# Moving the second MLP's tokens from byte 448 to byte 256 of each chunk of the activations

## The chip, the cores and the metric

The kernel runs on one core of a Trainium2 chip. The metric is the time of one execution on the device, in microseconds; the runs before the change are given as the median of three.

The engines are named as the profile names them: PE is TensorE's matmuls, PEld its weight loads, DVE is VectorE, ACT is ScalarE, POOL is GpSimd, SP is the queue that issues most transfers.

## The reference

Two transformer layers over 256 latent tokens and 256 context tokens of width 1024, batch 1. Layer 0 mixes with a retention scan, layer 1 with neighbourhood attention; both are followed by an MLP with 4096 hidden columns. The result is the latent tokens after layer 1.

```python
def sq_relu_mlp(h, w1, w2):
    return jnp.square(jax.nn.relu(h @ w1)) @ w2

# in each layer i, behind its mixer's output y:
x = layer_norm(DN_ALPHA * x + g1 * y, ln_g[i, 0], ln_b[i, 0])
h = x * (1.0 + sc2) + sh2
x = layer_norm(DN_ALPHA * x + g2 * sq_relu_mlp(h, mlp_w1[i], mlp_w2[i]), ln_g[i, 1], ln_b[i, 1])
```

In layer 0 the context tokens go through the MLP as well; in layer 1 only the 256 latent tokens do. The change concerns `h` of layer 1's MLP, "the second MLP".

## The kernel before

**Numbers in two parts.** Every matrix product is made of three matmuls on operands split into a high part (rounded to the chip's `float32r`) and a low part (the rest): high x high, high x low and low x high (`mm3`). Weights arrive by transfers of 512 KB (`fetch`, on the SP queue) into tiles `raw`; ScalarE casts them to `hi`, VectorE subtracts to get `lo` (`lows`). They are consumed in a fixed order (`take`).

**The activations.** The modulated tokens that a layer's products read stand transposed in two tiles, `hTh` (high) and `hTl` (low), of shape 128 partitions x 8 chunks x 512 columns. A chunk holds 128 of the 1024 features, one per partition, and its 512 columns are tokens: 2048 bytes in each partition. `hs(k, a, b)` gives columns a to b of chunk k of both. In the first MLP and in layer 1's mixer columns 0 to 255 are latent tokens and 256 to 511 context tokens.

**The second MLP's tokens.** They are only 256, so half of each chunk stays unused. `AT` (line 1928) is the column of the first of them, and `toks(t)` the columns of token tile t (128 tokens). `LINE` is 16 columns, 64 bytes. The columns are written by `affine_half` for token tile 0 (a ScalarE cast into `hTh`, a VectorE subtraction into `hTl`) and by `direct` for token tile 1.

**How they are read.** The first product of the second MLP has two forms:

- Hidden columns 0 to 511 (block 0) are made with the tokens as stationary operand, loaded as weights of 128 columns, and the MLP's weights as moving operand of 256 columns (`tok_part`, tiles `p1t`): 96 matmuls, interleaved by hand with the layer norm of the second token tile. Their results are transposed by `turn_block` (tiles `pt`).
- Hidden columns 512 to 4095 (blocks 1 to 7, the loop over `f4`) are made by `mm1`, with a 128 x 128 block of the MLP's weights as stationary operand and all 256 tokens as moving operand. Per block there are two halves `f2`, per half two groups of 128 hidden columns, 8 chunks and three matmuls: 7 x 2 x 2 x 8 x 3 = 672 matmuls into PSUM tiles that the profile calls `p`.

The first MLP calls the same `mm1` with `at=0`: for its first two blocks with the 256 latent tokens alone, then with all 512.

```python
def hs(k, a, b):
    return hTh[:, k, a:b], hTl[:, k, a:b]

def mm1(us, sl, pb, ks=range(KC), at=0):
    for i in range(2):
        for k in ks:
            wh, wl = us[k // 4]
            mm3(
                pb[i][:, sl], (wh[:, k % 4, tsl(i)], wl[:, k % 4, tsl(i)]),
                hs(k, at + sl.start, at + sl.stop), k == 0, k == KC - 1,
            )
```

A weight tile here is 128 partitions x 4 x 256 columns of 4 bytes, so the slice `wh[:, k % 4, tsl(i)]` starts 1024 (k % 4) + 512 i bytes into the tile. In the program's address map `hTh` starts at byte 40608 of each partition, `hTl` at 56992, and the five `hi` tiles at 97952 and steps of 4096 from there: all of them 160 bytes past a multiple of 512, as are the `lo` tiles.

**Order.** From the end of the mixer to the opening of the second MLP's loop the order of the instructions on PE, ACT, DVE and POOL is the written one; inside the loop the scheduler of the language orders what is ready. Behind the first product the second one (`mm2b`) reads the hidden values, not `hTh` or `hTl`, and the last layer norm and the output's transfers end the kernel.

Of the kernel before, what the change touches and what calls it, by code (L numbers as in the profile page):

```python
# [36 lines left out]
LINE = 16  # L37
# [67 lines left out]
def kernel(  # L105
# [50 lines left out]
    def bank(s="ps"):  # L156
        return psp.tile([P, 512], F32, tag="ps", name=nm(s))

    def slot(i, shape, dt, s):

        return arena.tile(shape, dt, tag=f"s{i}", name=nm(s))
# [1087 lines left out]
# [8 lines that stand above are left out]
# [668 lines left out]

    AT = 7 * LINE
    ht = slot(N_Q, [P, 4, 2, NLAT], F32R, "hid1")
    us4 = take(2, 0, 1)  # L1930

    def toks(t):
        return slice(AT + t * P, AT + (t + 1) * P)

# [126 lines left out]
    for f4 in range(1, 8):  # L2061
        ht = slot(HS1[f4], [P, 4, 2, NLAT], F32R, "hid1")
        for f2 in range(2):
            opening = f4 == 1 and f2 == 0
            us = take(2, 0, 2) if opening else take(2)
            pb = [bank("p1") for _ in range(2)]
            mm1(us, LAT, pb, at=AT)
            dve.on = f4 < 3
# [144 lines left out]
```

## Time and profile before

| | |
|---|---|
| median of three runs | 1175.99 us |
| lowest, highest | 1175.35, 1176.32 us |
| the profiled execution | 1176.32 us |
| its span, first to last instruction | 1174.4 us |
| granted TensorE clock, mean | 0.998 |

How the rows of the profile are read. In a group of instructions "x224: 276/276/369" is the count and the minimum, median and maximum duration in ns, followed by the first and last start in us and the shapes. Rows of the timeline give start and duration in us. Matmuls are pipelined, so their durations overlap; the distance between two starts is the time that a matmul costs. Rows of a window give, for each engine, busy us and in brackets the number of instructions, then the granted clock, the busy share of the DMA engines and GB/s. Rows of the chain give start, length, and what the chain ran through. All rows carry line 84 (L84), the helper that records every operation, so tiles tell them apart.

### The profile page before, as it was taken

To read this page: it belongs to the slowest core of one execution; us is meant where nothing else is said; L and a number is where in the kernel's file an instruction comes from. 1 tells how busy PE (TensorE), PEld (TensorE's weight loads), DVE (VectorE), ACT (ScalarE), POOL (GpSimd) and SP (SyncE) were. 2 spreads that over 40 slices of the span, in tenths; PEclk is the share of its full clock that TensorE was granted. 3 is DMA by queue.
4 is the path that set the end of the run, shared out by engine and by line. 5 is a ranking of instruction groups with operands and counts; after the bars stand their busy time and mean duration, and the time that the engine had idled before them with its cause. 6 is when DMAs were issued, how large, how long until landed. Compare 5 with 4: busy or idle time off the path is not lost.

```text
span 1174.4 us, 17544 instructions
## 1 busy us (share of the span) xinstructions
PE 1161.8 (99%) x6687; PEld 980.7 (84%) x6687; DVE 848.4 (72%) x1361; ACT 481.1 (41%) x819; POOL 235.1 (20%) x418
## 2 busy tenths in 40 slices
PE   9999999999999999999999999999999999999997
PEld 6788888888888889888888888879778878999886
DVE  3786687777898787757777675578577589877456
ACT  3643332222323246441212333137466666756341
POOL 0102001010220241770312001223443430000001
PEclk9999999999999999999999999999999999999999
DMA  9943552544355426756556665646344335766760
GB/s 275 277 130 105 162 187 96 156 153 144 112 178 177 140 65 220 181 113 215 177 184 198 211 200 179 197 157 202 81 136 144 107 113 160 214 206 205 237 215 36
DMA packets 140115, 195.10 MB, mean 166 GB/s; under 512 B 9936, under 2 KB 81136, under 8 KB 140032
## 3 DMA queue, kind: packets, MB, share of 16 engines
q1 hardware_dynamic: 131904, 182.03, 49.8%
q0 software_dynamic: 6976, 9.39, 3.8%
q10 hardware_dynamic: 1152, 2.56, 0.7%
q8 instruction: 52, 0.85, 0.3%
q14 instruction: 31, 0.25, 0.1%
HBM read 189.12 MB, written 5.75 MB: 166 GB/s over the span
## 4 chain that ended last, share of the span: by engine, by line
PE 74%; DMA 12%; DVE 8%; issue 3%; ACT 2%; POOL 0%; DVEq 0%; ACTq 0%
PE p L84 23%; DMA rawa<-in_ada_w_dram 11%; PE pq L84 8%; PE pv L84 8%; PE pw L84 7%; PE pg L84 7%; PE pn L84 4%; DVE acc L84 4%; PE pnv L84 4%; PE po L84 3%; DVE lo L84 3%; PE pnw L84 1%; PE ppt L84 1%; PE pS L84 1%; PE pav L84 1%
## 5 line engine op out<-in xcount | busy, mean ns | idle before, releaser
L84 ACT CAST hi<-raw 128x1024 fp32r<-128x1024 f32 (+2 forms) x228 | 231.9, 1032 | 306.7 <-PE p L84 114.2
L84 DVE TENSOR_TENSOR lo<-raw,hi 128x1024 fp32r<-128x1024 f32 (+2 forms) x228 | 272.6, 1210 | 101.3 <-ACT hi L84 101.1
L84 PE MATMUL p<-hi,hid 128*128 128x512 f32 (+1 forms) x780 | 238.2, 386 | 0.0
L84 PEld LDWEIGHTS p<-hi,hid 128*128 128x128 f32 x780 | 145.7, 188 | 29.3
L84 PE MATMUL p<-hTl,hi 128*128 128x256 f32 (+1 forms) x512 | 165.9, 326 | 0.0
L84 PE MATMUL p<-hTh,lo 128*128 128x256 f32 (+1 forms) x512 | 165.9, 326 | 0.0
L84 PE MATMUL p<-hTh,hi 128*128 128x256 f32 (+1 forms) x512 | 162.6, 327 | 0.0
L84 PE MATMUL p<-lo,hid 128*128 128x512 f32 (+1 forms) x390 | 150.8, 387 | 2.1 <-DVE lo L84 2.1
L84 DVE SCALAR_TENSOR_TENSOR acc<-rawa,scol,acc 128x1024 f32<-128x1024 f32 x56 | 74.4, 1341 | 65.1 <-DMA rawa<-in_ada_w_dram 65.1
L84 PEld LDWEIGHTS p<-hTh,lo 128*128 128x128 f32 x512 | 96.3, 188 | 8.8
L84 PEld LDWEIGHTS p<-hTl,hi 128*128 128x128 f32 x512 | 96.4, 188 | 8.7
L84 PEld LDWEIGHTS p<-hTh,hi 128*128 128x128 f32 x512 | 94.3, 188 | 8.7
L84 PEld LDWEIGHTS p<-lo,hid 128*128 128x128 f32 x390 | 73.3, 188 | 17.9 <-DVE lo L84 3.2
L84 DVE SCALAR_TENSOR_TENSOR strips<-rawa,scol,strips 128x512 f32<-128x512 f32 x112 | 78.6, 764 | 0.0
L84 ACT CAST hid<-r 128x256 fp32r<-128x256 f32 (+1 forms) x64 | 31.9, 500 | 112.4 <-DVE r L84 112.3
L84 POOL TENSOR_TENSOR rstd<-rstd,misc 128x1 f32<-128x1 f32 x28 | 19.1, 684 | 216.5 <-DVE rstd L84 215.5
L84 ACT ACTIVATE s<-s,mn 128x512 f32<-128x512 f32 x64 | 45.5, 713 | 21.6 <-DVE mn L84 21.6
L84 PE MATMUL pw<-hi,oh 128*128 128x512 f32 x128 | 50.8, 397 | 0.0
L84 PE MATMUL pg<-hi,hTh 128*128 128x512 f32 x128 | 50.6, 395 | 0.0
L84 PE MATMUL pw<-hi,ol 128*128 128x512 f32 x128 | 50.0, 390 | 0.0
L84 PE MATMUL pg<-hi,hTl 128*128 128x512 f32 x128 | 49.9, 390 | 0.0
L84 PE MATMUL pw<-lo,oh 128*128 128x512 f32 x128 | 49.8, 389 | 0.0
(241 smaller groups left out, 2275.2 us busy)
## 6 DMA issues: line engine op xcount, KB each, us to landing
raw<-in_mlp_w_dram SPq DMA_DIRECT2D x128, 512.0 KB, 4.5
rawa<-in_ada_w_dram SPq DMA_DIRECT2D x80, 512.0 KB, 3.9
raw<-in_ret_w_in_dram SPq DMA_DIRECT2D x42, 512.0 KB, 4.0
raw<-in_nat_w_in_dram SPq DMA_DIRECT2D x24, 512.0 KB, 4.1
rawq<-in_ada_w_dram SPq DMA_DIRECT2D x16, 512.0 KB, 6.0
raw<-in_ret_w_o_dram SPq DMA_DIRECT2D x16, 512.0 KB, 3.5
bias<-rpb_rows POOLq DMA_DIRECT2D x32, 128.0 KB, 2.9
raw<-in_nat_w_o_dram SPq DMA_DIRECT2D x8, 512.0 KB, 3.7
```

Of the source, the lines that this page charges most:

```text
L84: r = f(*args, **kwargs)
```

## The change

`AT` goes from 7 lines to 4: the tokens start 256 bytes into each chunk in place of 448, as columns 64 to 319 in place of 112 to 367. Both tiles, all eight chunks, every write and every read of them go along. Nothing else differs.

```diff
-    AT = 7 * LINE
+    AT = 4 * LINE
     ht = slot(N_Q, [P, 4, 2, NLAT], F32R, "hid1")
     us4 = take(2, 0, 1)
```

## The prediction

> **What bounds the kernel now.** I read the page first (busy shares, granted clock), then the chain of waits over the last 174 us, because the changed offset is first used at about 988 us, then the two stages that read the moved tokens, tile by tile and in order of time.
>
> ```profile
> span 1174.4 us, 17544 instructions
> PE 1161.8 (99%) x6687; PEld 980.7 (84%) x6687; DVE 848.4 (72%) x1361; ACT 481.1 (41%) x819; POOL 235.1 (20%) x418
> ...
> 1002.74 5.66 PE p L84 x48
> 1008.40 0.44 PE pt L84 x4
> 1008.83 158.03 PE p L84 x1026
> 1166.87 0.02 issue
> ```
>
> TensorE is busy 99% of the span. The other rows are the chain in order of time: from 1002.74 to 1166.87 us it is TensorE alone (matmuls into `p`, once broken by four transposes), and behind that only a short settling of the last outputs. So a matmul that issues later in this stretch ends the kernel later, one for one.
>
> ```profile
> core 0: us, PE busy (x) PEld busy (x) DVE busy (x) ACT busy (x) POOL busy (x), PEclk, DMA share, GB/s
> 1010.00:1079.00 69.00, 69.00 (x611) 69.00 (x611) 54.64 (x84) 42.25 (x76) 0.00 (x0) 1.00 0.65 204
> ...
> L84 PE MATMUL p<-hTh,hi x224: 276/276/369, 1002.5 to 1079.1; 128*128 128x256 f32 x112
> ```
>
> This is the first product of the second MLP (blocks 1 to 7 of its hidden columns): 224 matmuls for each of the three pairs of high and low parts, of which the row shows one, 672 in all, of 256 tokens each, from 1002.5 us until the second product takes over at 1079.4. In the window TensorE never idles at a granted clock of 1.00, while VectorE is busy 54.64 of 69 us, ScalarE 42.25 and the DMA engines 0.65. The median duration is 276 ns, but matmuls overlap; what counts is the distance from start to start.
>
> **The change part by part.** The change alters one constant, so no instruction, DMA, queue entry or wait is added or removed. Every pair of accesses that overlapped before overlaps still (the earlier readers of these two tiles read all 512 token columns of a chunk), so the waits are the same. What moves is an address: columns 112 to 367 of each chunk become columns 64 to 319, 192 bytes lower. Four groups touch them.
>
> *1. The 672 matmuls, which stream these tokens as moving operand.* Each runs with a weight load of 128 columns beside it, out of a tile whose slices start at multiples of 512 bytes; in the program's address map the token tiles and all weight tiles of this product start 160 bytes past a multiple of 512. So the starts of the two streams differ by 448 modulo 512 now, and by 256 after. The first MLP runs the same form of matmul with the tokens at offset 0, which gives a pair of rows to compare: first the old stage at offset 0, then this one.
>
> ```profile
> 450.43 0.28 PE L84 MATMUL p<-hTh,lo 128*128 128x256 f32 x1
> ...
> 450.91 0.28 PE L84 MATMUL p<-hTh,lo 128*128 128x256 f32 x1
> ...
> L84 PE MATMUL p<-hTh,hi x27: 283/283/283, 447.1 to 455.0; 128*128 128x256 f32 x27
> L84 PEld LDWEIGHTS p<-hTl,hi x20: 192/192/192, 447.1 to 454.0; 128*128 128x128 f32 x20
> ```
>
> ```profile
> 1040.19 0.28 PE L84 MATMUL p<-hTh,lo 128*128 128x256 f32 x1
> ...
> 1041.89 0.28 PE L84 MATMUL p<-hTh,lo 128*128 128x256 f32 x1
> ...
> L84 PE MATMUL p<-hTh,hi x178: 276/276/276, 1011.7 to 1071.9; 128*128 128x256 f32 x178
> L84 PEld LDWEIGHTS p<-hTl,hi x177: 187/188/188, 1012.1 to 1071.9; 128*128 128x128 f32 x177
> ```
>
> At offset 0 four steps (450.43 to 450.91, three rows left out) take 0.48 us: 120 ns each, every matmul lasts 283 ns and every weight load 192. At offset 448 fifteen steps (1040.19 to 1041.89) take 1.70 us: 113.3 ns each, the matmul 276, the load 187 to 188. Same shape, same clock, no idle time in either: only the offset differs, and it is worth 6.7 ns per matmul. The rows at offset 0 also bound the pattern: that stage uses weight slices 0, 512, 1024 ... bytes into a tile, and minimum, median and maximum are all 283. So a shift of 512 bytes changes nothing, and only the offset modulo 512 can matter. One more row belongs here, from the start of the same stage, still at offset 448:
>
> ```profile
> 1005.05 0.28 PE L84 MATMUL p<-hTh,hi 128*128 128x256 f32 x1
> ...
> 1006.23 0.28 PE L84 MATMUL p<-hTl,hi 128*128 128x256 f32 x1
> ...
> L84 PE MATMUL p<-hTh,hi x13: 281/281/281, 1002.9 to 1007.2; 128*128 128x256 f32 x13
> ```
>
> Ten steps in 1.18 us are 118 ns (the chain's first piece, 48 matmuls in 5.66 us, says the same: 117.9), at 281 ns a matmul. So 448 itself has two rhythms: the first 48 matmuls run in the slow one, and behind the four transposes at 1008.4 us the other 624 run in the fast one. Which one is taken seems to hang on how the two streams stand to one another when TensorE starts afresh.
>
> What 256 does, no row shows; I bound it. From below: transposes of 128 columns load the same number of weight columns, and their rhythm is the least one that any full-width load shows.
>
> ```profile
> 1002.14 0.60 PE L84 MATMUL pt<-cst,r 128*128 128x128 f32 x4
> ...
> L84 PE MATMUL pt<-cst,r x8: 270/272/273, 1002.1 to 1008.6; 128*128 128x128 f32 x8
> ```
>
> Four of them span 0.60 us, the last of which lasts 0.272, so three steps take 0.33 us: 109 ns. From above: 120 ns, the slowest steady rhythm that a matmul of 256 tokens has anywhere in the trace. Between 109 and 120 I take 120. The fewest assumptions that give 448 a gain over 0 are that the two streams disturb each other by place, in a pattern that repeats after some number of bytes. It repeats at 512. If it also repeats at 256 or 128, then 256 is the same as 0, while 448, which is a multiple of 64 alone, remains different. Only if it repeats at 512 and nowhere below is 256 a new case. The row that 256 is nearest to is the one at offset 0.
>
> The cost: 624 x 6.7 ns = 4.2 us, and 48 x (120 - 117.9) = 0.1 us. All of it is on the chain.
>
> [...]
>
> *2. The 96 matmuls of block 0, which load these tokens as weights* (moving the weights of the model instead, 989 to 1002 us).
>
> ```profile
> 989.38 0.62 PE L84 MATMUL p1t<-hi,hTh 128*128 128x256 f32 x4
> 989.84 0.62 PE L84 MATMUL p1t<-lo,hTh 128*128 128x256 f32 x4
> 990.29 0.96 PE L84 MATMUL p1t<-hi,hTh 128*128 128x256 f32 x7
> ...
> L84 PE MATMUL p1t<-hi,hTh x32: 276/279/392, 989.4 to 998.7; 128*128 128x256 f32 x32
> ```
>
> Eight steps from 989.38 to 990.29 take 0.91 us, again 113 to 114 ns; the median over all is 279 ns, so most run near the 281 of the slow rhythm. At 120 ns some 16 matmuls lose 6.7 ns and 80 lose about 2.1: 0.3 us. At the floor of 109 they would gain 16 x 4.3 + 80 x 8.9 = 0.8 us.
>
> *3. The writes into the moved columns.*
>
> ```profile
> L84 ACT CAST hTh<-aff x2: 621/622/622, 987.8 to 989.9; 128x512 fp32r<-128x512 f32 x2
> ...
> L84 ACT CAST hTh<-aff x8: 601/618/641, 783.3 to 807.6; 128x512 fp32r<-128x512 f32 x8
> ```
>
> At 448 the cast takes 621 ns; the same form in the second layer's mixer, at other columns, takes 618. Medians 3 ns apart: I cost these two at nothing, and with them the four subtractions and the eight small affine writes of the second token tile; at 3 ns each all 14 are under 0.05 us either way.
>
> *4. What runs beside it.* A slower TensorE gives the weight transfers, casts and subtractions more room, so no wait arises. A faster one would ask 4% more of engines that are busy at most 79% in that window; nothing new is late there. The second product that follows, up to 1166.9 us, does not read these tiles and moves as a block.
>
> The sum is 4.2 + 0.1 + 0.3 = 4.6 us. The profiled execution took 1176.32 us (1.9 us around its span of 1174.4), which gives 1180.9; it is the highest of the three runs, 0.33 above their median of 1175.99, so I predict 1180.6 us, 0.4% slower. The three runs lie within 0.08%; I count 0.2% (2.35 us) as what can be told from no change.
>
> **The rivals.**
> *Offset 256 behaves as 448 does.* Any offset that is no multiple of 512 may part the two streams as well. For it: 448 helps in two roles, as moving operand (1040 us) and as weights (989 us), where the shift has the opposite sign, so the gain does not hang on one direction. Against it: two rhythms at one and the same offset show that details matter. Time: 1176.0; if all 672 take the fast rhythm, 48 x 4.6 ns = 0.2 less. [...]
> *Offset 256 keeps the streams apart for good.* In one step of 120 ns 256 columns are streamed and 128 loaded, so the moving stream reads at twice the pace of the weight stream: from equal starts it is a whole 512-byte turn ahead just as both end, and meets the other stream at each boundary. Started half a turn apart they would meet only in mid-stream. The point that decides is whether such a meeting costs under 4 ns. Price: 624 x 4.3 + 48 x 8.9 = 3.1 us, with part 2's 0.8 in all 3.9 us: 1172.1, down to which the other engines in the window keep up. [...]
> *Offset 256 locks into the slow rhythm throughout*: 624 x 4.6 = 2.9 us, 1178.9.
> *The mid-stream meeting is expensive*, the moving stream being held behind the slower one: beyond 120 ns, which no row of the trace shows; each 10 ns would be 6.7 us.
>
> **How the numbers follow.** As offset 0 (1180.6): 0.46. As 448 (1176.0): 0.25. Floor or near it (1172.1 to 1173.6): 0.18. Slow rhythm throughout (1178.9): 0.07. Beyond 120 ns: 0.04. The likeliest case alone lies within 1179.9 to 1181.3 (the three runs' spread to both sides). The cases have both signs, so the range goes from the floor case to that upper end, 1172.0 to 1181.3, and leaves out only the last. Slower by over 0.2%: 0.46 + 0.07 + 0.04 = 0.57; within 0.2%: 0.25 and a little of the floor case that stops short, 0.27; faster: 0.16.
>
> **What would show it.** In the stage after 1002 us, start to start of 120 ns, matmuls of 283 ns and loads of 192 show the first step right; 276 and 113.3 show the first rival, 272 to 273 and 109 the second, 281 the third. The stage of 672 should last 81 us in place of 76.9, and everything before 988 us and each step behind the stage should keep its length. The prediction is wrong if the pattern of the two streams has no period below 512 bytes.

## The result and the profile after

| | before | after |
|---|---|---|
| median of seven runs | 1175.64 us | 1180.94 us |
| lowest, highest | 1172.57, 1177.92 us | 1177.42, 1182.74 us |
| the profiled execution, its span | 1176.32, 1174.4 us | 1182.74, 1180.8 us |

The ratio is 1.0040 with a 95% interval of 1.0026 to 1.0054: 3.1 to 6.3 us slower. On every engine the instructions are the same, in number and in order.

The page of the changed kernel opens with its span and the busy shares:

```profile
span 1180.8 us, 17544 instructions
PE 1168.2 (99%) x6687; PEld 986.2 (84%) x6687; DVE 849.5 (72%) x1361; ACT 482.9 (41%) x819; POOL 234.9 (20%) x418
```

TensorE's matmuls are busy for 6.4 us more, as much as the span grew; VectorE and ScalarE gained 1.1 and 1.8 us. Where the 6.4 us lie is read from the chain of waits, in order of time (start, length, what), first of the kernel after, then the rows of the kernel before that the prediction did not show:

```profile
988.75 2.87 PE pnw L84 x24
991.62 1.92 PE p1t L84 x16
...
993.57 1.79 PE p1t L84 x12
...
996.35 8.16 PE p1t L84 x68
1004.51 0.44 PE pt L84 x4
1004.94 5.76 PE p L84 x48
1010.70 0.44 PE pt L84 x4
1011.14 162.18 PE p L84 x1026
```

```profile
986.67 2.89 PE pnw L84 x24
...
990.39 1.06 ACT hi L84
...
991.49 1.78 PE p1t L84 x12
...
994.28 8.03 PE p1t L84 x68
```

The last piece grew from 158.03 to 162.18 us. It holds 624 matmuls of the moved tokens and 402 of the second product, so that is 4.15 / 624 = 6.65 ns for each of the 624. The first 48 grew from 5.66 to 5.76 us, block 0's 68 from 8.03 to 8.16. The transposes between them kept their 0.44. That makes 4.4 us. Block 0's first 28 matmuls add almost nothing: from the end of `pnw` to the piece of 68 it is 4.72 us before and 4.73 after. In the kernel before TensorE waited behind the first 16 of them for a cast on ScalarE (`ACT hi`); after, the 16 run longer and the wait is gone. The remaining 2 us are there before the changed offset is used: this execution enters the chain at 988.75 in place of 986.67. They are taken up below.

The stage itself, by a window, by tile, and in order of time, as the prediction read it of the kernel before:

```profile
1012.00:1085.00 73.00, 73.00 (x610) 73.00 (x609) 56.00 (x85) 44.83 (x78) 0.00 (x0) 1.00 0.64 196
```

```profile
L84 PE MATMUL p<-hTh,hi x181: 283/283/283, 1014.9 to 1079.7; 128*128 128x256 f32 x181
L84 PEld LDWEIGHTS p<-hTl,hi x181: 192/192/192, 1014.9 to 1079.7; 128*128 128x128 f32 x181
```

```profile
1040.00 0.28 PE L84 MATMUL p<-hTh,lo 128*128 128x256 f32 x1
...
1041.80 0.28 PE L84 MATMUL p<-hTh,lo 128*128 128x256 f32 x1
```

Still no idle time at a granted clock of 1.00, and VectorE, ScalarE and the transfers are about as busy as before (77, 61 and 64% against 79, 61 and 65%). Fifteen steps take 1.80 us in place of 1.70: 120.0 ns each, every matmul 283 ns, every load 192. These are the numbers of the first MLP at offset 0, to the nanosecond.

**The 2 us that are not the change's.** Both executions wait near 768 us for the low part of a weight tile, behind late transfers of weights: the cast on ScalarE that comes ahead of it waited 4.97 us for its transfer before and 5.43 us after. The chain just behind the waits, before and then after:

```profile
770.33 9.62 PE p L84 x41
```

```profile
769.44 12.55 PE p L84 x47
```

The two pieces do not begin at the same matmul, since the kernel before waits a second time, shortly. The matmul that starts at 768.23 us before starts at 769.44 after, 1.2 us later; 0.56 us of that is the longer idle stretch ahead of it, the rest was there before. At the transposes at the end of these pieces, 779.94 and 781.98 us, the kernel after is 2.04 us late. The windows show where the other 0.8 us come from (the seventh figure behind the stretch, ahead of the DMA share, is the granted clock), before and then after; below them are the rows of the two waits:

```profile
768.20:770.30 2.10, 1.66 (x6) 1.05 (x6) 1.96 (x7) 1.05 (x1) 0.51 (x1) 1.00 1.02 289
```

```profile
766.00:769.40 3.40, 1.17 (x6) 0.63 (x4) 3.34 (x6) 1.04 (x1) 0.00 (x0) 1.00 0.70 197
769.40:772.80 3.40, 3.36 (x8) 2.69 (x9) 3.26 (x8) 1.04 (x1) 0.51 (x1) 0.51 0.91 289
```

```profile
768.23 0.50 PE L84 MATMUL p<-lo,hid 128*128 128x512 f32 x1 [1.70 <-DVE lo L84]
```

```profile
769.44 0.79 PE L84 MATMUL p<-lo,hid 128*128 128x512 f32 x1 [2.26 <-DVE lo L84]
```

Behind an idle stretch of 2.26 us the granted clock was 0.51 for 3.4 us, eight matmuls long; behind one of 1.70 us it stayed at 1.00. The wait lies in the first layer's MLP, which no moved column touches, and it is not in every run: in the profiled run of the experiment with a later break (below) one piece of the chain passes over the place, 161 matmuls in 36.50 us, the 226.7 ns of an unbroken stream.

The 2.26 us stand in a stretch of 3.40 us, 766.00 to 769.40, of which TensorE was busy for 1.17. In the profiled run of the experiment at 480 bytes (below) two waits in the same place, 1.9 us together and the longer one 1.4, left the clock at 1.00 in the windows from 764 to 776 us.

### The profile page after: what moved, and what is told of

It is laid out like the page before. It is cut to its first block, busy times and chain, and to the rows that moved or that the text cites. A ratio compares the mean times of both kernels' runs of the same rounds, so it can differ in the third digit from the quotient of the medians.

```text
span 1180.8 us, 17544 instructions
## 1 busy us (share of the span) xinstructions
PE 1168.2 (99%) x6687; PEld 986.2 (84%) x6687; DVE 849.5 (72%) x1361; ACT 482.9 (41%) x819; POOL 234.9 (20%) x418
## 4 chain that ended last, share of the span: by engine, by line
PE 74%; DMA 13%; DVE 8%; issue 2%; ACT 1%; SPq 1%; POOL 0%; DVEq 0%; ACTq 0%
PE p L84 24%; DMA rawa<-in_ada_w_dram 11%; PE pg L84 7%; PE pw L84 7%; PE pq L84 7%; PE pv L84 6%; PE pn L84 5%; PE pnv L84 4%; DVE acc L84 4%; PE po L84 3%; DVE lo L84 3%; PE ppt L84 2%; PE pnw L84 1%; PE pS L84 1%; PE pav L84 1%
## 5 line engine op out<-in xcount | busy, mean ns | idle before, releaser
L84 PE MATMUL pq<-hTh,hi 128*128 128x512 f32 x128 | 49.3, 395 | 0.8 <-ACT hTh L84 0.4
```

The lines of the kernel that those rows point to most:

```text
L84: r = f(*args, **kwargs)
```

## The experiments

The theory: what counts is the difference between the start of the moving operand and the start of the weights, in a pattern that repeats every 256 bytes. Its rivals: a pattern that repeats every 128 bytes; the place of the tokens alone, whatever the weights' place; and, for the two rhythms seen at 448, that the order of the work decides more than the bytes. No kernel here leaves out any computation. All edits are to the changed kernel, and each group was timed beside the kernel before on its chip (medians 1175.14, 1175.14 and 1175.47 us). "The stage" is the 672 matmuls; the chain's two pieces `p x48` and `p x1026` measure it, and per matmul the last 624 take 113.3 ns plus what the second piece has over 158.03 us, divided by 624.

**Offset 0: is 256 the same as 0?**

```diff
-    AT = 4 * LINE
+    AT = 0
```

> The changed kernel with the tokens at the start of each chunk. Theories A, A' and B: the same as 256, 120 ns in the stage of 672 and in block 0, matmuls of 283 ns, 1180.6 us, ratio to the kernel before about 1.004. If 256 and 0 differ by more than 0.1% or by more than 1 ns a matmul, the reading that 256 repeats 0 falls.

Measured: 1179.89 us, ratio 1.0044 (1.0025 to 1.0064). The chain, and the tile in the stage:

```profile
1005.81 5.76 PE p L84 x48
...
1012.01 162.18 PE p L84 x1026
```

```profile
L84 PE MATMUL p<-hTh,hi x154: 283/283/283, 1019.8 to 1074.8; 128*128 128x256 f32 x154
```

5.76 and 162.18 us, 283 ns: the same three numbers as at 256. A shift by 256 bytes changes none of them here.

**Offset 128: does the pattern repeat at 128?**

```diff
-    AT = 4 * LINE
+    AT = 2 * LINE
```

> The changed kernel with the tokens 128 bytes into each chunk in place of 256. Theory A (the moving stream and the weight load disturb each other by the difference of their starts, in a pattern that repeats every 128 bytes): as 256, 120 ns from start to start and matmuls of 283 ns in the stage of 672, time as the changed kernel, about 1180.6 us. Theory A' (the pattern repeats every 256 bytes, not every 128): 128 is a case of its own, at or below 118 ns, matmuls of 281 ns or less, 1176 to 1179 us. Theory B (where the tokens lie, not how they stand to the weights, sets it) leaves both open. Theory C (the state in which TensorE starts the stage picks the rhythm, the offset only tips it): a mix of 113, 118 and 120 ns within the stage.

Measured: 1180.27 us, ratio 1.0056 (1.0036 to 1.0075); the chain's second piece is 162.22 us, a mean of 120.0 ns. By the mean alone 128 would pass for 0. The tile, form by form, says otherwise:

```profile
L84 PE MATMUL p<-hTh,lo x84: 284/284/285, 1044.8 to 1074.6; 128*128 128x256 f32 x84
L84 PE MATMUL p<-hTh,hi x84: 285/285/285, 1044.9 to 1074.8; 128*128 128x256 f32 x84
L84 PE MATMUL p<-hTl,hi x84: 281/281/282, 1045.0 to 1074.9; 128*128 128x256 f32 x84
```

284, 285 and 281 ns in turn, where offset 0 has 283 for each; start to start the three steps take 118 to 122 ns. So the pattern does not repeat at 128, though the time is the same. Neither expectation came out whole: a pattern of 128 was to give 283 ns throughout, one of 256 at most 118 ns.

**Offset 64.**

```diff
-    AT = 4 * LINE
+    AT = 1 * LINE
```

> The changed kernel with the tokens 64 bytes into each chunk. Theories A and A': an odd multiple of 64 bytes, so 113.3 or 117.9 ns as at 448, and about 1176 us (1176 to 1179 if it stays in the 117.9 ns rhythm); if 448 was good because it is just below 512 and not because it is an odd multiple, 120 ns and 1180.6 us. Theory C: rhythm as in the changed kernel where the start of the stage is the same, 120 ns.

Measured: 1177.85 us, ratio 1.0025 (1.0011 to 1.0038).

```profile
993.39 7.87 PE p1t L84 x68
...
1001.70 5.66 PE p L84 x48
...
1007.79 160.81 PE p L84 x1026
```

```profile
L84 PE MATMUL p<-hTl,hi x157: 279/279/279, 1019.8 to 1074.9; 128*128 128x256 f32 x157
```

The second piece has 2.78 us more than at 448, 4.5 ns per matmul: all 672 run at 117.8 ns, the mean of the slow rhythm that 448 shows in its first 48 alone (though a matmul lasts 279 ns here and 281 there), and the transposes do not end it. Block 0, where the tokens are the weights, gains instead: 7.87 us for 68 matmuls, against 8.03 at 448 and 8.16 at 256. There the difference of the two streams has the opposite sign, so 64 stands in block 0 as 192 does in the stage, and 448 (192 modulo 256) as 64. For these 68 matmuls the order of the times is swapped with the roles: 115.7 ns on the mean at 64, 118.1 at 448. For block 0's first 16 it is not, here at 64:

```profile
988.50 0.63 PE L84 MATMUL p1t<-hi,hTh 128*128 128x256 f32 x4
...
989.44 1.90 PE L84 MATMUL p1t<-hi,hTh 128*128 128x256 f32 x12
```

Eight steps take 0.94 us, about 117.5 ns, where the prediction's rows of block 0 at 448 have 113 to 114. So the fast rhythm occurs at a difference of 64 too, and the difference alone does not say which of the two rhythms is taken.

**The weight tiles moved, the tokens left at 256.** A tile of 64 bytes ahead of the weight tiles shifts them, and what lies behind them, up by 64. The difference becomes 192 modulo 256, as it is at 448, while the tokens stay in their columns.

```diff
+    padp = ec(tc.tile_pool(name="padp", bufs=1))
     hip = ec(tc.tile_pool(name="hip", bufs=WB))
...
+    padp.tile([P, 16], F32, tag="pad", name="pad")
```

> The changed kernel, tokens still at 256, with 64 unused bytes ahead of the weight tiles, so that all weight tiles (and the tiles placed behind them) lie 64 bytes higher and the token tiles stay. Theory A and A' (the difference of the two starts counts): the stage of 672 goes back to 113.3 or 117.9 ns although the tokens lie where the changed kernel has them, and so does every other stage of 256 token columns against weights (120 ns before): minus 4 to 5 us there, and for the 512-column matmuls of the token tiles either nothing (226.7 ns) or up to 6.7 ns each (220 ns). Theory B (the tokens' own place counts): the stage of 672 stays at 120 ns and the time at 1180.6 us. Theory C: no rhythm changes but by chance.

Measured: 1184.3 us, ratio 1.0086 (1.0068 to 1.0103): slower than everything so far. The chain and the tile in the stage:

```profile
1012.75 5.66 PE p L84 x48
...
1018.84 158.04 PE p L84 x1026
```

```profile
L84 PE MATMUL p<-hTl,hi x163: 276/276/276, 1019.8 to 1074.9; 128*128 128x256 f32 x163
```

In the stage the kernel before is back: 5.66, then 158.04 us, 276 ns. The tokens' own place alone is not what counts. The loss lies elsewhere: the matmuls of 512 columns, in the first layer, now meet weights 64 bytes further on. In order of time, in the first MLP, before and then here:

```profile
469.80 0.39 PE L84 MATMUL p<-hTl,hi 128*128 128x512 f32 x1
...
473.88 0.39 PE L84 MATMUL p<-hTl,hi 128*128 128x512 f32 x1
```

```profile
469.81 0.39 PE L84 MATMUL p<-hTl,hi 128*128 128x512 f32 x1
...
474.01 0.39 PE L84 MATMUL p<-hTl,hi 128*128 128x512 f32 x1
```

Eighteen steps take 4.08 us before, 226.7 ns each, and 4.20 us here, 233.3. The same move that is worth 6.7 ns to a matmul of 256 columns costs one of 512 columns 6.7 ns, which the expectation had not allowed for (it had no change or a gain). That MLP has 672 of them (4.5 us), and the projections, which read the same tiles, slow as well: the matmuls into `pq` between 341 and 351 us take 226.7 ns from start to start before and 233.3 here.

**Offset 192, which is 448 modulo 256.**

```diff
-    AT = 4 * LINE
+    AT = 3 * LINE
```

> The changed kernel with the tokens 192 bytes into each chunk. If the pattern of moving start minus weight start repeats every 256 bytes, 192 is 448: 113.3 ns in the stage of 672 (with a stretch of 117.9 ns at its start), near 118 ns in block 0, and the time of the kernel before, ratio 1.000 within 0.2%. If it repeats at 512 alone, 192 is one more case, between 109 and 120 ns, and agreeing with 448 to the ns would be chance.

Measured: 1175.46 us, ratio 1.0006 (0.9986 to 1.0027), no change from the kernel before.

```profile
1002.02 5.66 PE p L84 x48
...
1008.11 158.03 PE p L84 x1026
```

5.66 and 158.03 us, the numbers of 448 in both places, the break at the transposes included. With offset 0 this makes two pairs 256 bytes apart that agree to 0.01 us.

**Offsets between the lines of 64 bytes: 480 and 416.**

```diff
-    AT = 4 * LINE
+    AT = 120
```

> The changed kernel with the tokens 480 bytes into each chunk, half a line of 64 bytes from 448 towards 512. If places count in whole steps of 64 bytes, it repeats one of its neighbours, 113.3 ns (448) or 120 ns (512), 1176 or 1180.6 us. If the pattern is finer, a value of its own; the floor of the trace is 109 ns, which would be 1172 us.

```diff
-    AT = 4 * LINE
+    AT = 104
```

> The changed kernel with the tokens 416 bytes into each chunk, 32 bytes below 448: a start difference of 160 modulo 256, between 128 (120.0 ns on average, three different steps) and 192 (113.3 or 117.8). If 32 bytes matter as at 480 (224: 118.3 ns, uneven steps), between 113 and 120 with uneven steps; if places count in lines of 64 bytes of the address map, in which all tiles start 32 bytes into a line, it falls together with 384 or with 448. Stage 77 to 81 us, time 1176 to 1180.

Measured: 1179.07 us, ratio 1.0041 (1.0021 to 1.0061) at 480 bytes, and 1178.24 us, ratio 1.0026 (1.0014 to 1.0038) at 416. The chain's second piece and the tile in the stage, at 480 and then at 416:

```profile
1007.91 161.15 PE p L84 x1026
```

```profile
L84 PE MATMUL p<-hTh,hi x142: 277/280/285, 1019.8 to 1069.9; 128*128 128x256 f32 x142
```

```profile
1009.38 160.55 PE p L84 x1026
```

```profile
L84 PE MATMUL p<-hTh,hi x157: 277/280/282, 1019.8 to 1074.7; 128*128 128x256 f32 x157
```

118.3 and 117.3 ns on the mean, in uneven steps (277 to 285 ns a matmul) instead of one value. Half a line of 64 bytes to either side of 448 loses more than half of what 448 has over 256, so 448 stands on a narrow best place and not on a slope. Its own slow rhythm, 117.8 ns, lies between theirs: what is narrow is the place at which the stage took the fast rhythm behind the transposes.

**448 without the break at the transposes.** The transposes of block 0's results are moved ahead of the loop, so that nothing interrupts the 672.

```diff
-    AT = 4 * LINE
+    AT = 7 * LINE
...
     r11 = activate(p11)
+    turn_block(r10, 1, 0)
+    turn_block(r11, 1, 1)
...
-                if opening and i == 0:
-                    turn_block(r10, 1, 0, hid[0])
-                    turn_block(r11, 1, 1, hid[0])
```

> The kernel before (tokens at 448) with the transposes that interrupt the stage of 672 behind its 48th matmul moved ahead of it. If the rhythm is set where TensorE starts afresh and kept until the next interruption, all 672 run in the rhythm in which they start: 117.9 ns throughout (80 us in place of 76.9 for the stage, plus 2.9 us) or 113.3 throughout (minus 0.2 us). If the stream drifts into the fast rhythm by itself, 113.3 for nearly all of it and no change of the time beyond the few hundred ns of the moved transposes.

Measured: 1180.37 us, ratio 1.0055 (1.0034 to 1.0076). The chain, the tile in the stage, and the window ahead of it:

```profile
1003.00 166.47 PE p L84 x1074
```

```profile
L84 PE MATMUL p<-hTh,hi x157: 281/281/282, 1019.8 to 1074.9; 128*128 128x256 f32 x157
```

```profile
985.00:1003.00 18.00, 16.21 (x134) 15.48 (x134) 16.11 (x32) 13.37 (x31) 0.93 (x1) 1.00 0.55 173
```

All 672 stay in the slow rhythm, 281 ns: 166.47 us against 5.66 + 158.03 = 163.69, which is 2.78 us more, 4.5 ns for each of 624. Most of the rest of the loss is idle time ahead of the stage, 1.79 of the 18 us against 0.13 in the kernel before, in which TensorE waits for block 0's results; the expectation had put the moved transposes at a few hundred ns.

**448 with the break later.** The same transposes, put behind the 144th matmul of the stage.

```diff
-    AT = 4 * LINE
+    AT = 7 * LINE
...
-                if opening and i == 0:
+                if f4 == 2 and f2 == 0 and i == 0:
```

> The kernel before (tokens at 448) with the four transposes that interrupt the stage of 672 placed behind its 144th matmul in place of its 48th. If the interruption sets the rhythm: 117.9 ns up to the 144th matmul and 113.3 ns for the 528 behind it, so 96 x 4.6 ns = 0.4 us more than the kernel before, which the times cannot tell. If the stream finds the fast rhythm by itself after some 5 us, or if the rhythm in the kernel without the interruption came from the later start, the change of rhythm does not fall on the transposes.

Measured: 1176.38 us, ratio 1.0013 (1.0002 to 1.0024).

```profile
999.24 16.97 PE p L84 x144
1016.20 0.44 PE pt L84 x4
1016.64 147.15 PE p L84 x930
```

The first piece takes 16.97 us for 144 matmuls, 117.8 ns each; the second has 96 matmuls fewer than the 158.03 us of before and is 10.88 us shorter, 113.3 ns each. The rhythm changes where the transposes stand, and nowhere else. At a difference of 192 both rhythms hold, 117.8 and 113.3 ns, and the four transposes changed the one for the other. What makes it choose is not shown.

**Which load disturbs?** Beside a matmul the trace records the load of the next matmul's weights: in the kernel before, the load for the matmul `p<-hTh,lo` of 1040.19 us stands at 1040.08, where the matmul ahead of it starts. To tell that load from the matmul's own, high and low were given different differences: low weight tiles 64 bytes higher, high tokens at 448, low tokens at 256.

```diff
-    AT = 4 * LINE
+    AT = 7 * LINE
+    padp = ec(tc.tile_pool(name="padp", bufs=1))
     lop = ec(tc.tile_pool(name="lop", bufs=WB))
...
+    padp.tile([P, 16], F32, tag="pad", name="pad")
...
-    def hs(k, a, b):
-        return hTh[:, k, a:b], hTl[:, k, a:b]
+    DL = 3 * LINE
+
+    def hs(k, a, b, d=0):
+        return hTh[:, k, a:b], hTl[:, k, a - d : b - d]
...
```

The second MLP's reads pass `d=DL`, and its writes of the low tokens go 192 bytes lower; the other reads keep `d=0`.

> The low weight tiles (and what is placed behind them) lie 64 bytes higher; high tokens at 448, low tokens at 256. The order is high tokens on high weights, low tokens on high weights, high tokens on low weights. Start differences modulo 256 of a matmul and its own weights: 192, 0, 128; of a matmul and the weights that are loaded beside it, which are the next one's: 192, 192, 192. If the stream is disturbed by the load that runs beside it, all 672 run as at 448: 113.3 ns (117.9 in the first stretch). If it were the own weights, a third runs fast and two thirds at 120: a mean of about 118 with three different steps. The total time is not compared: other products change their places as well.

Measured in one run: 1194.78 us. Most of the loss lies ahead of the stage: the chain's `pnw x24` starts at 999.35 us, against 986.67 in the kernel before. That the moved weight tiles cost it, by matmuls of 512 columns as above, is the author's estimate. The chain's second piece takes 163.93 us; 624 matmuls at the mean below are 73.8 of them, which leaves 90.1 us for the 402 of the second product, by estimate, against 87.3 before. So that piece does not measure this stage alone. The stage, in order of time and by tile:

```profile
1045.82 0.28 PE L84 MATMUL p<-hTh,lo 128*128 128x256 f32 x1
...
1048.66 0.28 PE L84 MATMUL p<-hTh,lo 128*128 128x256 f32 x1
```

```profile
L84 PE MATMUL p<-hTh,lo x100: 278/282/283, 1044.7 to 1079.9; 128*128 128x256 f32 x100
```

Twenty-four steps take 2.84 us: 118.3 ns on the mean, in uneven steps (278 to 283 ns a matmul in this group alone). Neither reading appears in its clean form. The map below gives 117.8 to 119.3 ns for the one that counts a matmul's own weights (192, 0 and 128 in turn), and 118.3 lies within that. It is also within 0.5 ns of the slow rhythm of 192, 117.8 ns, which the other reading allows as well, but in even steps. One run in which three differences alternate does not settle it. It stays open.

**The map.** By the difference of the moving operand's start from the weights', modulo 256 bytes:

| difference | offsets that show it | ns per matmul of the stage | time, us |
|---|---|---|---|
| 0 | 0, 256 | 120.0, even | 1179.89, 1180.94 |
| 64 | 64 | 117.8, even | 1177.85 |
| 128 | 128 | 120.0, three steps of 118 to 122 | 1180.27 |
| 160 | 416 | 117.3, uneven | 1178.24 |
| 192 | 192, 448, and 256 with the weights 64 higher | 117.8, or 113.3 behind a restart | 1175.46, 1175.64, (1184.3) |
| 224 | 480 | 118.3, uneven | 1179.07 |

None of these beats the kernel before. In block 0, where the roles are swapped, the fast rhythm occurs at a difference of 64 too.

## Why the prediction was right, and where it was not

**Step 1, the 672 matmuls (4.2 + 0.1 us): right, and for its reason.** The last 624 went from 113.3 to 120.0 ns (4.15 us measured), the first 48 from 117.9 to 120.0 (0.10). The step rested on taking 256 for the same as 0. Offset 0 run in this very stage has the same chain pieces to 0.01 us (5.76 and 162.18), and 192 repeats 448 (5.66 and 158.03), so in both pairs the pattern repeats after 256 bytes. The other leg, that the difference to the weights counts, is shown by the moved weight tiles: tokens still at 256, and 113.3 ns again. The prediction left open whether the period was 256 or 128; the three unequal matmuls at offset 128, 284, 285 and 281 ns, say 256. The eight offsets run have five different means, from 113.3 to 120.0 ns. What in the chip makes the difference count, no run shows.

**The two rhythms of 448: seen rightly, then used too lightly.** The prediction supposed that a fresh start chooses between them; the two runs with the transposes moved bear it out for 448: 117.8 ns up to the transposes and 113.3 behind them, and 117.8 for all 672 where they stand ahead. What it did not draw from this is that only 2.2 ns of the 6.7 lie in the bytes alone, and 4.5 in the restart. Without the four transposes in the loop the change would have cost some 672 x 2.2 ns = 1.5 us in the stage, by estimate: 256 was not run without them. The sum came out right because the offset was changed and the order was not.

**Step 2, block 0 (0.3 us): right in sign, twice too large.** The chain shows 0.13 us in the 68 matmuls. The first 16, 1.92 us in the chain of after, do run at 120 ns in place of 113 to 114, but the 0.1 us that the prediction charged for them reached the chain with 0.01: the kernel before spent it waiting for ScalarE.

**Step 3, the writes (nothing): right.** The cast takes 620 to 622 ns, as at 448.

**Step 4, nothing beside it: right.** The window above has the other engines about as busy as before, and what follows the chain's last piece keeps its length: 7.5 us to the end of the span in both.

**The sum.** 4.6 us forecast, 4.4 in the chain. The two medians of seven differ by 5.3 and the ratio's interval reaches from 3.1 to 6.3. The forecast of 1180.6 lies within 0.4 us of the median, which is closer than the runs can tell: that much of it is luck.

**What was off.** That "everything before 988 us" should keep its length failed in the profiled execution, by 2 us: 1.2 us of waits up to 769 us and 0.8 at the clock drop behind them. The prediction also took the three runs' 0.08% for the scatter; seven runs of each kernel scatter by 0.45%, 5.3 us, as much as the two medians differ. So its likeliest case's own range, 1179.9 to 1181.3, was narrower than single runs can be. The difference was settled by the chain of one execution and the ratio over many, not by any two times.

**The rivals.** "256 behaves as 448" and "256 keeps the streams apart" fall at once by 283 ns and 120.0. The second had taken its floor of 109 ns from the transposes, which stream 128 columns; no offset here reached it with 256: 113.3 is the least. "The slow rhythm throughout" exists, at 448 without the break and at 64 in place of 256, and at 64 it gave 1177.85 us where the prediction had worked out 1178.9. "Beyond 120 ns" appears at no offset on the mean.

## What to carry to other kernels

When TensorE has no idle time in a stage and the granted clock is 1.00, as here, read the distance from start to start, and compare it between stages that run the same form of matmul on operands at different places: 113.3 against 120.0 ns with no idle time was here a matter of where the operands lie, and 672 matmuls made 4 us of it. Judge a place by the difference to the other operand, in every stage that uses either tile: the difference that took matmuls of 256 columns from 120.0 to 113.3 ns took those of 512 from 226.7 to 233.3. And look at what interrupts the stream: the slow rhythm of 448, 117.8 ns, lasted here until the transposes, 48 or 144 matmuls, and through all 672 without them.

## What the runs showed of the hardware that was not expected

- At 256 columns the rhythm went with the difference of the two operands' starts, from 113.3 to 120.0 ns, and repeated after 256 bytes in the two pairs run, 0 with 256 and 192 with 448. At 512 columns, where two differences were compared, the order is the opposite: 226.7 ns at a difference of 0, 233.3 at 192.
- At one and the same difference two steady rhythms exist, 113.3 and 117.8 ns: at 192 in the stage, at 64 in block 0. Four transposes in the stage switched from the slow one to the fast one at 192, behind the 48th matmul as behind the 144th; at 64 they switched nothing.
- 32 bytes made a difference: 416 and 480 run at 117.3 and 118.3 ns, in uneven steps, beside the 113.3 of 448.
- The granted clock fell to 0.51 for 3.4 us behind an idle stretch of 2.26 us, and was 1.00 behind stretches of 1.70 and, in another run, 1.4 us.
